# Deferred evictions and outputs of a squared-ReLU MLP tied in emission order; rows of the next block loaded further ahead

## The chip, the cores and the metric

One NeuronCore of one Trainium2 chip runs the whole layer. The metric is the device time of one execution in microseconds (us), as the median of the runs; less is better.

## What is computed

One step of a one-layer hybrid decoder in float32, for a prompt of 2048 tokens and for 8 x 8 sample tokens, 2112 rows in all. A token mixer (dilated attention, a Mamba-2 scan and a short gated convolution, with one input and one output projection) is followed by the MLP, the part that the change touches:

```python
x = x + rms_norm(mix, norm_mix_post[l])
h = rms_norm(x, norm_mlp_pre[l])
f = jnp.square(jax.nn.relu(h @ w_mlp_up[l])) @ w_mlp_down[l]   # 1024 -> 4096 -> 1024
x = x + rms_norm(f, norm_mlp_post[l])
```

## The kernel before

**Engines.** PE is the matrix engine (TensorE), DVE the vector engine, ACT the scalar engine, POOL the general engine GpSimd, SP the engine that only issues transfers. In the code they are `PE`, `V`, `A`, `G` and `SP`. Each works through its own instructions in order. The program is emitted by Python loops, and a scheduler then places the instructions of each engine; `tc.issue_after(ins)` keeps what is emitted under it behind `ins` in that placing. `Last` wraps an engine and remembers the last instruction emitted on it (`V.last`, `G.last`).

**Precision.** Every float32 operand is split in two rounded halves, `hi` and `lo`, and each product is made of three matmuls (hi·lo, lo·hi, hi·hi; `mm3`). So each weight tile costs ACT a cast (`whi`) and a subtraction (`wlo`: POOL's for up weights, DVE's for down weights), and each activation tile costs ACT a cast (`shi`) and DVE a subtraction (`slo`).

**Tiling.** The MLP runs from about 1340 us to the end, in three blocks of 704 rows. A block is two halves of 352 rows, each in three row pieces (128, 128 and 96 rows, p = 0 to 2). Up and down projections are each made by seven products in place of eight: first the up products in the order 1, 2, 6, 7, 5, 3, 4, then the down products in the order 1, 2, 7, 4, 5, 6, 3. Each product has eight steps (`jj`), 56 up and 56 down a block. An up step is 24 matmuls, 352 wide; a down step is 18 matmuls, 512 wide, two tiles `j` of nine: for each of the three banks wlo·shi and whi·shi, then three times whi·slo.

**One turn of the main loop** (a step `at`) emits the load of the weights four steps ahead (`w_load`, SP), the split of the weights one step ahead (`w_split`), a deferred piece of work if there is one (`late`), the activations of the next down step (`down_split`: DVE makes the combination `x`, then `shi` and `slo`), and then the matmuls of the step. The split weights lie in eight buffers, so the splits of a step wait until PE is done with the step two before it.

**At the end of a down product** its three PSUM banks (`pm`) are added into the output rows `Y` by DVE (`down_out`, rows y1 and y2 of the two halves): two additions a row piece for product 5, three for product 6. Where y2 is whole, ACT squares it (`jkf`, two a row piece) for the norm. For products 5 and 6 row piece 0 is done at once; row pieces 1 and 2 go to the list `late`, from which each turn takes one. `mlp_out` writes a finished row piece: POOL adds the sums of squares (`ssf`) and makes the reciprocal root (`rstd_ms`, `rstd`), DVE scales two halves of 512, POOL issues the transfer to `out_y_prompt`, which accumulates. y2 is written in steps 2 to 4 of product 3; y1 goes through `late` (`finish`) and is written in the first up steps of the next block.

**Rows of the next block.** The generator `half` has SP load three row tiles (`xt`), yields a number (a lead in us of PE's work), and then transposes them on PE (`pq`), with ACT copying each result (`q`). Transfers and transposes stand in between the steps as the streams are polled.

Of the kernel before, what the change touches and what calls it, by code (L numbers as in the profile page):

```python
# [2 lines left out]

# [1 line left out]

# [138 lines left out]
@with_exitstack  # L144
def hybrid_layer(ctx: ExitStack, tc: tile.TileContext, I, O, stage=9):
    nc = tc.nc
    V, A, G, PE, SP = Last(nc.vector), nc.scalar, Last(nc.gpsimd), TimedPE(nc.tensor), Last(nc.sync)

    cpool = ctx.enter_context(tc.tile_pool(name="const", bufs=1))
    dpool = ctx.enter_context(tc.tile_pool(name="scratch", bufs=1, space=DRAM))  # L150
# [150 lines left out]
    def y_rows(t0, n):  # L301
        if t0 < S:
            return O["y_prompt"][0, t0:t0 + n, :]
        return O["y_sample"].rearrange("b s d -> (b s) d")[t0 - S:t0 - S + n, :]
# [1303 lines left out]
    def s_pair(src):  # L1608

        hi = s4.tile([P, HT], F32R, name="shi", tag="s")  # L1610
        lo = s4.tile([P, HT], F32R, name="slo", tag="s")
        A.copy(hi, src)  # L1612
        V.tensor_sub(lo, src, hi.bitcast(F32))
        return hi, lo
# [109 lines left out]
    def up_sums(b):  # L1724

        (q11, q12), (q21, q22) = halves[b, 0].q, halves[b, 1].q

        def each(f):
            for c in range(4):
                with tc.issue_after(V.last):  # L1730
                    f(c)
                yield 3.0

        yield from each(lambda c: V.tensor_sub(q21[c], q21[c], q22[c]))
        while len(up_s.get((b, 1), [])) < 4:
            yield 1.0
        yield from each(lambda c: V.tensor_sub(q11[c], q21[c], q11[c]))
        src.update({(b, 6): q11, (b, 5): q21, (b, 4): q22})
        while len(up_s.get((b, 2), [])) < 4:
            yield 1.0  # L1740
        yield from each(lambda c: V.scalar_tensor_tensor(q12[c], q12[c], -1.0, q11[c], op0=ALU.mult,
                                                         op1=ALU.subtract))
        src[b, 3] = q12
# [16 lines left out]
    def down_split(b, i, j):  # L1760
        with tc.issue_after(V.last):
            a = down_form(i, j)
        down_s[b, i, j] = s_pair(a)

    def down_form(i, j):
        x = {k[:2]: v for k, v in X.items() if k[2] == j}
        if i == 1:
            a = x[1, 1]
        elif i == 2:
            a = x[1, 2]  # L1770
        elif i == 7:
            a = t4.tile([P, HT], F32, name="d3", tag="t")
            V.tensor_sub(a, x[1, 1], x[2, 1])
        elif i == 4:
            a = x[2, 2]
        elif i == 5:
            a = x[2, 1]
            V.tensor_sub(a, a, x[2, 2])
        elif i == 6:
            a = x[1, 1]  # L1780
            V.tensor_sub(a, x[2, 1], a)
        else:
            a = x[1, 2]
            V.scalar_tensor_tensor(a, a, -1.0, x[1, 1], op0=ALU.mult, op1=ALU.subtract)
        return a
# [36 lines left out]
    def mlp_out(b, t, p, last=False):  # L1822

        a, n = TP[p]
        t0 = BT * b + HT * (t - 1) + a
        y, ss = Y.pop((t, p)), SS.pop((t, p))
        G.tensor_add(ss[:n, 0:1], ss[:n, 0:1], ss[:n, 1:2])
        r = rstd_of(e4, ss[:, 0:1], n, D)
        for d in range(2):
            cs = slice(512 * d, 512 * d + 512)  # L1830
            o = y[:n, cs]
            if last and d == 0:
                A.activation(o, o, AF.Copy, scale=r[:n])
            else:
                with tc.issue_after(V.last):
                    V.scalar_tensor_tensor(o, o, r[:n], g4[:n, cs], op0=ALU.mult, op1=ALU.mult)
        for t1, t2 in ((t0, min(t0 + n, S)), (max(t0, S), t0 + n)):
            if t1 < t2:
                G.dma_start(y_rows(t1, t2 - t1), y[t1 - t0:t2 - t0], accum_op=ALU.add)
# [6 lines left out]
    def half(b, t):  # L1846
        h = halves[b, t] = Half(b, t, XT if b else [(y4, "y")])
        h.rows()
        yield 12.0
        yield from h.turn(psT, "tr")  # L1850

    def second_half(b):
# [3 lines left out]
    def next_block(b):  # L1856
        yield from half(b, 1)
        yield 6.0
        yield from half(b, 0)
        src[b, 1], src[b, 2] = halves[b, 0].q  # L1860
        yield from up_sums(b)

    late = []

# [3 lines left out]
    for at, (kind, b, i, jj) in enumerate(steps):  # L1868
        if at + 4 < len(steps):
            w_load(at + 4)  # L1870
        while nsplit[0] < len(steps) and nsplit[0] <= at + (2 if idle_y(nsplit[0]) else 1):
            w_split(nsplit[0])
            nsplit[0] += 1
        order = UP_ORDER if kind == "u" else DOWN_ORDER
        nxt = steps[at + 2] if at + 2 < len(steps) else None

        if kind == "u" and jj == NJ // 2 - 2 and i != UP_ORDER[-1]:
            ni = UP_ORDER[UP_ORDER.index(i) + 1]
            up_split(b, ni, (0, 1, 2))
        if kind == "d" and i == DOWN_ORDER[-1] and jj == NJ // 2 - 1 and (b + 1, 1) in src:  # L1880
            up_split(b + 1, 1, (0, 1, 2))
        if late:
            late.pop(0)()

        two = steps[at + 1] if at + 1 < len(steps) else None
        if two is not None and two[0] == "d" and kind == "d":
            for j2 in range(2):
                down_split(two[1], two[2], 2 * two[3] + j2)
        if kind == "u":
            hi, lo = wts.pop(at)  # L1890
            s = up_s[b, i]
            for j2 in range(2):
                ps = bank()
                for c in range(4):
                    ws = slice(2 * P * c + P * j2, 2 * P * c + P * j2 + P)
                    mm3(ps[:, :HT], hi[:, ws], lo[:, ws], *s[c], c == 0, c == 3)
                up_out(i, 2 * jj + j2, ps)
        else:
            hi, lo = wts.pop(at)
            if jj == 0:  # L1900
                banks = [bank() for _ in TP]
            for j2 in range(2):
                j = 2 * jj + j2
                s = down_s.pop((b, i, j))
                ws = slice(512 * j2, 512 * j2 + 512)
                for p, (a, n) in enumerate(TP):
                    mm3(banks[p][:n], s[0][:, a:a + n], s[1][:, a:a + n], hi[:, ws], lo[:, ws], j == 0, j == NJ - 1)
            if jj == NJ // 2 - 1:
                for p in range(len(TP)):
                    if i in (5, 6) and p:  # L1910
                        late.append(lambda i=i, p=p, ps=banks[p]: end_tile(i, p, ps))
                    else:
                        end_tile(i, p, banks[p])
        if two is not None and two[0] == "d" and kind == "u":
            for j2 in range(2):
                down_split(two[1], two[2], 2 * two[3] + j2)
        if kind == "u" and jj == NJ // 2 - 1 and i != UP_ORDER[-1]:
            up_split(b, UP_ORDER[UP_ORDER.index(i) + 1], (3,))
        if kind == "d" and i == DOWN_ORDER[-1] and jj == NJ // 2 - 1 and b + 1 < TT // BT:
            while (b + 1, 1) not in src:  # L1920
                advance(min(streams, key=lambda st: st[1]))
            have = len(up_s.get((b + 1, 1), []))
            up_split(b + 1, 1, range(have, 4))
        if kind == "d":
            end, last = jj == NJ // 2 - 1, b == TT // BT - 1
            if i == 2 and end and last:
                for p in range(len(TP)):
                    o = Y[1, p][:TP[p][1], :512]
                    V.tensor_mul(o, o, g4[:TP[p][1], :512])
            if i == 3 and not end and 2 <= jj < 2 + len(TP):  # L1930
                mlp_out(b, 2, jj - 2)
            if i == 3 and end:
                def finish(p, b=b, last=last):
                    square(1, p, 2)
                    mlp_out(b, 1, p, last)
                for p in range(len(TP)):
                    if last:
                        finish(p)
                    else:
                        late.append(lambda p=p, f=finish: f(p))  # L1940
        if kind == "d" and i == 5 and jj == 4 and b + 1 < TT // BT:
            stream(next_block(b + 1))
        if at % 20 == 10 and shifts:
            nm, sr, sb_ = shifts.pop(0)
            with tc.issue_after(wload[0].ins):
                SP.dma_start(O[nm][0, sb_, 0:WB - NS].rearrange("t h e -> t (h e)"),
                                  I[sr][0, sb_, NS:WB].rearrange("t h e -> t (h e)"))
        poll()
# [38 lines left out]
```

## Time and profile before

| | us |
|---|---|
| runs | 2785.82, 2782.39, 2784.89 |
| median | 2784.89 |
| the profiled execution: its time | 2779.39 |
| its span, first to last instruction | 2777.6 |
| PE busy | 2577.4 (93%) |
| DVE, ACT, POOL busy | 1509.1, 1328.9, 1087.9 |
| mean granted TensorE clock | 0.969 |

All numbers of the profile are from that one execution, which lies 5.5 us below the median of the runs. The views used are the page of the profile (busy time of each engine), the same in chosen stretches of time, the waits of an engine with what ended each of them, and the timeline of single instructions. A timeline row has start and duration in us, engine, line, operation, the tile written and those read, the shape, a count where several like ones are joined, and in brackets the idle time before it with what released it. Matmuls are pipelined, so one shown with 0.39 us can follow another after 0.23 us.

### The profile page before, as it was taken

What the parts mean: (1) busy time and instruction counts of PE and PEld (TensorE: products, weight loads), DVE (VectorE), ACT (ScalarE), POOL (GpSimd) and SP (SyncE); (2) the same over time, 40 slices, a digit from 0 to 9 for tenths busy, and PEclk for the clock granted to TensorE, in tenths of its full rate; (3) what the DMA queues carried; (4) which work ended last, traced back from release to release, by engine and by line L of the source; (5) the groups of instructions that cost most, each with busy time, mean ns of one, the idle gap of its engine ahead of it and who ended that gap; (6) DMA issues with size and microseconds to landing.
All of it is one profiled execution on the core that took longest, in us unless ns stands there. A gap on an engine that the chain in (4) does not pass through costs nothing. (4 is left out here: it accounts for less than half of the span.)

```text
span 2777.6 us, 40701 instructions
## 1 busy us (share of the span) xinstructions
PE 2577.4 (93%) x14329; PEld 2182.4 (79%) x14329; DVE 1509.1 (54%) x2994; ACT 1328.9 (48%) x2776; POOL 1087.9 (39%) x1008
## 2 busy tenths in 40 slices
PE   7998889989999878999999999999999999999996
PEld 6898767877877755556799977689987779998775
DVE  4555536455456465554154466754546674445676
ACT  4534334435436333334456644454764455385443
POOL 4545444444354544434577300066610017660002
PEclk9999899999999988999999999999999999999998
DMA  7777998777677649978776545374534456543343
GB/s 206 221 184 225 271 245 241 202 212 217 182 212 198 163 134 285 279 225 265 239 234 203 151 155 169 127 228 167 167 122 153 131 161 210 167 160 132 125 152 87
DMA packets 426260, 528.26 MB, mean 190 GB/s; under 512 B 65482, under 2 KB 326130, under 8 KB 421448
## 3 DMA queue, kind: packets, MB, share of 16 engines
q1 hardware_dynamic: 411352, 483.45, 54.7%
q0 software_dynamic: 14704, 42.21, 9.1%
q8 instruction: 113, 1.85, 0.3%
q14 instruction: 91, 0.75, 0.1%
HBM read 447.90 MB, written 178.19 MB: 225 GB/s over the span
## 5 line engine op out<-in xcount | busy, mean ns | idle before, releaser
L137 POOL TENSOR_TENSOR wlo<-wraw,whi 128x512 fp32r<-128x512 f32 (+2 forms) x359 | 675.5, 1909 | 522.2 <-ACT whi L417 292.6
L1604 ACT CAST whi<-wraw 128x1024 fp32r<-128x1024 f32 x336 | 351.8, 1049 | 334.4 <-PE pm L118 272.2
L118 PE MATMUL pm<-slo,whi 128*128 128x352 f32 x1344 | 436.0, 326 | 7.9 <-DVE x2t L137 3.5
L118 PE MATMUL pm<-shi,wlo 128*128 128x352 f32 x1344 | 432.2, 327 | 8.6 <-POOL wlo L137 8.6
L118 PE MATMUL pm<-shi,whi 128*128 128x352 f32 x1344 | 437.3, 325 | 0.0
L118 PE MATMUL pm<-wlo,shi 128*128 128x512 f32 (+1 forms) x1008 | 398.7, 396 | 1.0 <-ACT shi L1612 1.0
L118 PE MATMUL pm<-whi,shi 128*128 128x512 f32 (+1 forms) x1008 | 397.9, 395 | 0.0
L118 PE MATMUL pm<-whi,slo 128*128 128x512 f32 (+1 forms) x1008 | 340.1, 400 | 19.9 <-DVE slo L137 19.8
L137 DVE TENSOR_TENSOR wlo<-wraw,whi 128x1024 fp32r<-128x1024 f32 (+1 forms) x169 | 206.2, 1220 | 206.3 <-ACT whi L1604 192.6
L118 PE MATMUL pj<-lo,whi 128*128 128x512 f32 (+1 forms) x720 | 272.1, 378 | 17.6 <-ACT xr L631 8.2
L118 PEld LDWEIGHTS pm<-slo,whi 128*128 128x128 f32 x1344 | 255.5, 190 | 10.7 <-ACT whi L1604 4.0
L118 PE MATMUL pj<-hi,whi 128*128 128x512 f32 (+1 forms) x720 | 262.9, 365 | 0.0
L118 PEld LDWEIGHTS pm<-shi,wlo 128*128 128x128 f32 x1344 | 254.7, 190 | 9.4 <-POOL wlo L137 9.4
L118 PE MATMUL pj<-hi,wlo 128*128 128x512 f32 (+1 forms) x720 | 261.8, 364 | 0.0
L137 POOL TENSOR_TENSOR ssf<-ssf 128x1 f32<-128x1 f32 (+1 forms) x18 | 9.1, 503 | 643.0 <-ACT jkf L1820 642.8
L118 PEld LDWEIGHTS pm<-shi,whi 128*128 128x128 f32 x1344 | 255.4, 190 | 0.2
L137 DVE TENSOR_TENSOR x<-pm,x 128x352 f32<-128x352 f32 x240 | 123.7, 521 | 235.7 <-PE pm L118 235.4
L118 PEld LDWEIGHTS pm<-whi,slo 128*128 128x128 f32 (+1 forms) x1008 | 179.8, 181 | 75.7 <-DVE slo L137 26.4
L118 PEld LDWEIGHTS pm<-wlo,shi 128*128 128x128 f32 (+1 forms) x1008 | 182.3, 181 | 56.1 <-ACT shi L1612 4.1
L118 PEld LDWEIGHTS pm<-whi,shi 128*128 128x128 f32 (+1 forms) x1008 | 181.7, 180 | 51.2 <-issue 0.2
L1612 ACT CAST shi<-x 128x352 fp32r<-128x352 f32 x288 | 136.8, 484 | 164.9 <-DVE x L137 112.2
L137 DVE TENSOR_TENSOR slo<-x,shi 128x352 fp32r<-128x352 f32 x288 | 156.7, 554 | 35.8 <-ACT shi L1612 30.6
(324 smaller groups left out, 4856.9 us busy)
## 6 DMA issues: line engine op xcount, KB each, us to landing
wraw<-in_w_in SPq DMA_DIRECT2D x192, 256.0 KB
wraw<-u_d SPq DMA_DIRECT2D x96, 512.0 KB
wraw<-d_d SPq DMA_DIRECT2D x96, 512.0 KB
wraw<-in_w_mlp_up SPq DMA_DIRECT2D x72, 512.0 KB
wraw<-in_w_mlp_down SPq DMA_DIRECT2D x72, 512.0 KB
u_d<-in_w_mlp_up POOLq DMA_DIRECT2D x64, 256.0 KB, 5.7
d_d<-in_w_mlp_down POOLq DMA_DIRECT2D x64, 256.0 KB, 7.0
out_s_k<-in_cache_attn_k SPq DMA_DIRECT2D x8, 2040.0 KB
```

What stands on the lines that cost most here:

```text
L118: return self.eng.matmul(out, lhsT, rhs, **kw)
L137: out = f(*args, **kw)
L1604: A.copy(hi, raw)
L1612: A.copy(hi, src)
```

## The change

Four edits. The remembered last instruction is now kept for ACT too. The deferred work `late` is taken after `down_split` of the next step instead of before it, and everything that it emits is placed behind the last instructions emitted on DVE, ACT and POOL (`in_order`). The outputs of y2 are bound in the same way. And `half` yields 18 us in place of 12 between the loads and the transposes.

```diff
-    V, A, G, PE, SP = Last(nc.vector), nc.scalar, Last(nc.gpsimd), TimedPE(nc.tensor), Last(nc.sync)
+    V, A, G, PE, SP = Last(nc.vector), Last(nc.scalar), Last(nc.gpsimd), TimedPE(nc.tensor), Last(nc.sync)
...
         h.rows()
-        yield 12.0
+        yield 18.0
...
+    @contextmanager
+    def in_order():
+
+        with tc.issue_after(V.last), tc.issue_after(A.last), tc.issue_after(G.last):
+            yield
...
-        if late:
-            late.pop(0)()
 
         two = steps[at + 1] if at + 1 < len(steps) else None
         if two is not None and two[0] == "d" and kind == "d":
             for j2 in range(2):
                 down_split(two[1], two[2], 2 * two[3] + j2)
+        if late:
+            with in_order():
+                late.pop(0)()
...
             if i == 3 and not end and 2 <= jj < 2 + len(TP):
-                mlp_out(b, 2, jj - 2)
+                with in_order():
+                    mlp_out(b, 2, jj - 2)
```

The set of instructions is the same in both kernels; their order on the engines is not. SP's order is the same, and so are the places of the transposes on PE. Three places differ in the second half of each block.

DVE from product 5 to product 6 of block 0. Before (y are the evictions of product 5, x11 and slo the activations of product 6, wlo4 its weights; `slo_17684` is the second tile of its first step):

```order
L137 TENSOR_TENSOR y2_17155<-y2_17155,pm_17440 128x512
L137 TENSOR_TENSOR y1_16585<-y1_16585,pm_17440 128x512
L137 TENSOR_TENSOR x11_14399<-x21_15069,x11_14399 128x352
L137 TENSOR_TENSOR wlo4_17710<-wraw4_17603,whi4_17709 128x1024
L137 TENSOR_TENSOR y2_17157<-y2_17157,pm_17441 96x512
L137 TENSOR_TENSOR y1_16587<-y1_16587,pm_17441 96x512
L137 TENSOR_TENSOR slo_17684<-x11_14370,shi_17683 128x352
```

And now, from the same place:

```order
L137 TENSOR_TENSOR wlo4_17710<-wraw4_17603,whi4_17709 128x1024
L137 TENSOR_TENSOR x11_14387<-x21_15069,x11_14387 128x352
L137 TENSOR_TENSOR slo_17684<-x11_14356,shi_17683 128x352
L137 TENSOR_TENSOR slo_17715<-x11_14387,shi_17714 128x352
L137 TENSOR_TENSOR x11_14404<-x21_15084,x11_14404 128x352
L137 TENSOR_TENSOR wlo4_17749<-wraw4_17637,whi4_17748 128x1024
L137 TENSOR_TENSOR x11_14434<-x21_15106,x11_14434 128x352
L137 TENSOR_TENSOR slo_17720<-x11_14404,shi_17719 128x352
L137 TENSOR_TENSOR y2_17155<-y2_17155,pm_17440 128x512
L137 TENSOR_TENSOR y1_16585<-y1_16585,pm_17440 128x512
```

The four evictions of row pieces 1 and 2 moved from ahead of that slo to behind those of the next two steps (the two of row piece 0 stand ahead of it in both).

DVE from product 6 to product 3. Before (`slo_18007` is the second tile of product 3's first step, `slo_18058` the first of its second):

```order
L137 TENSOR_TENSOR y2_17153<-pm_17725,y2_17153 128x512 x2
L137 TENSOR_TENSOR y1_16583<-pm_17725,y1_16583 128x512
L137 TENSOR_TENSOR y2_17155<-pm_17726,y2_17155 128x512 x2
L137 TENSOR_TENSOR y1_16585<-pm_17726,y1_16585 128x512
L137 SCALAR_TENSOR_TENSOR x12_14051<-x12_14051,x11_14399 128x352
L137 TENSOR_TENSOR y2_17157<-pm_17727,y2_17157 96x512 x2
L137 TENSOR_TENSOR y1_16587<-pm_17727,y1_16587 96x512
L137 TENSOR_TENSOR wlo4_18045<-wraw4_17914,whi4_18044 128x1024
L137 SCALAR_TENSOR_TENSOR x12_14087<-x12_14087,x11_14446 128x352
L137 TENSOR_TENSOR slo_18007<-x12_14023,shi_18006 128x352
L137 TENSOR_TENSOR slo_18058<-x12_14051,shi_18057 128x352
```

And now, where these two tiles are `slo_18001` and `slo_18044`:

```order
L137 TENSOR_TENSOR y2_17153<-pm_17725,y2_17153 128x512 x2
L137 TENSOR_TENSOR y1_16583<-pm_17725,y1_16583 128x512
L137 TENSOR_TENSOR wlo4_18039<-wraw4_17908,whi4_18038 128x1024
L137 SCALAR_TENSOR_TENSOR x12_14051<-x12_14051,x11_14387 128x352
L137 TENSOR_TENSOR slo_18001<-x12_14023,shi_18000 128x352
L137 TENSOR_TENSOR wlo4_18090<-wraw4_17948,whi4_18089 128x1024
L137 TENSOR_TENSOR slo_18044<-x12_14051,shi_18043 128x352
L137 SCALAR_TENSOR_TENSOR x12_14066<-x12_14066,x11_14404 128x352
L137 SCALAR_TENSOR_TENSOR x12_14087<-x12_14087,x11_14434 128x352
L137 TENSOR_TENSOR slo_18049<-x12_14066,shi_18048 128x352
L137 TENSOR_TENSOR y2_17155<-pm_17726,y2_17155 128x512 x2
L137 TENSOR_TENSOR y1_16585<-pm_17726,y1_16585 128x512
```

Six evictions left the way of `slo_18001`, and the weights of the third step (`wlo4_18090`) came ahead of `slo_18044`.

ACT at the same place, now (`whi4_18089` are the weights of the third step, `shi_18043` is the first tile of the second; before, four squares stood ahead of that shi, and this whi behind it):

```order
L137 CAST whi4_18038<-wraw4_17908 128x1024
L137 CAST shi_18000<-x12_14023 128x352
L137 ACTIVATE jkf_18026,ssf_18025<-y2_17153 128x512
L137 ACTIVATE jkf_18028,ssf_18025<-y2_17153 128x512
L137 CAST whi4_18089<-wraw4_17948 128x1024
L137 CAST shi_18043<-x12_14051 128x352
L137 CAST shi_18048<-x12_14066 128x352
L137 CAST shi_18094<-x12_14087 128x352
L137 ACTIVATE jkf_18056,ssf_18055<-y2_17155 128x512
```

Here too the squares of row pieces 1 and 2 moved back, and a whi moved ahead of a shi.

POOL at the start of block 1, where y1 of block 0 is written between the weight splits of the first up product (`wlo4_18471` belongs to its third step, `wlo4_18517` to its fourth). Before:

```order
L137 TENSOR_TENSOR ssf_16855<-ssf_16855 128x1
L137 TENSOR_TENSOR ssf_16859<-ssf_16859 128x1
L137 TENSOR_SCALAR rstd_ms_18431<-ssf_16855 128x1
L137 TENSOR_TENSOR ssf_16863<-ssf_16863 96x1
L137 TENSOR_SCALAR rstd_ms_18477<-ssf_16859 128x1
L137 TENSOR_TENSOR rstd_18432<-rstd_ms_18431,mhalf_117 128x1
L137 TENSOR_SCALAR rstd_ms_18523<-ssf_16863 96x1
L137 TENSOR_TENSOR rstd_18478<-rstd_ms_18477,mhalf_117 128x1
L137 TENSOR_TENSOR rstd_18524<-rstd_ms_18523,mhalf_117 96x1
L137 TENSOR_TENSOR wlo4_18471<-wraw4_18295,whi4_18470 128x1024
L137 DMA out_y_prompt<-y1_16583 128x1024
L137 TENSOR_TENSOR wlo4_18517<-wraw4_18336,whi4_18516 128x1024
```

And now:

```order
L137 TENSOR_TENSOR ssf_16855<-ssf_16855 128x1
L137 TENSOR_SCALAR rstd_ms_18431<-ssf_16855 128x1
L137 TENSOR_TENSOR rstd_18432<-rstd_ms_18431,mhalf_117 128x1
L137 TENSOR_TENSOR wlo4_18471<-wraw4_18295,whi4_18470 128x1024
L137 TENSOR_TENSOR ssf_16859<-ssf_16859 128x1
L137 DMA out_y_prompt<-y1_16583 128x1024
L137 TENSOR_SCALAR rstd_ms_18477<-ssf_16859 128x1
L137 TENSOR_TENSOR wlo4_18517<-wraw4_18330,whi4_18516 128x1024
L137 TENSOR_TENSOR rstd_18478<-rstd_ms_18477,mhalf_117 128x1
L137 TENSOR_TENSOR ssf_16863<-ssf_16863 96x1
L137 TENSOR_SCALAR rstd_ms_18523<-ssf_16863 96x1
L137 TENSOR_TENSOR rstd_18524<-rstd_ms_18523,mhalf_117 96x1
```

The norms of row pieces 1 and 2 moved behind the splits of the third and fourth step; the other two transfers stood between the two splits before, and now stand behind the split of the fifth step (`wlo4_18563`).

More of the change, by code (lines that the diff above doesn't have):

```diff
@@ L1 @@
 import math
-from contextlib import ExitStack
+from contextlib import ExitStack, contextmanager
 import numpy as np
```

## The prediction

> **What bounds the kernel.** I read the page first, then stretches of 50 us, then TensorE's waits, then the timelines where it waits. In the rows by stretch, the five pairs after the length are busy time and instructions of PE, PEld, DVE, ACT and POOL; then come the granted TensorE clock, the DMA share and GB/s.
>
> ```profile
> PE 2577.4 (93%) x14329; PEld 2182.4 (79%) x14329; DVE 1509.1 (54%) x2994; ACT 1328.9 (48%) x2776; POOL 1087.9 (39%) x1008
> ```
>
> ```profile
> 1650.00:1700.00 50.00, 49.97 (x218) 38.56 (x217) 31.17 (x48) 22.78 (x36) 0.00 (x0) 1.00 0.42 127
> ...
> 1750.00:1800.00 50.00, 45.91 (x190) 35.29 (x190) 36.95 (x63) 23.81 (x43) 5.64 (x9) 0.93 0.32 107
> 1800.00:1850.00 50.00, 44.51 (x227) 39.83 (x226) 32.06 (x48) 25.78 (x45) 30.12 (x23) 0.93 0.75 205
> 1850.00:1900.00 50.00, 50.00 (x313) 50.00 (x312) 22.72 (x38) 30.90 (x56) 32.64 (x14) 1.00 0.70 231
> ```
>
> TensorE (PE) is the bound: 93% of the span, and 49.97 or 50.00 of 50 us where nothing disturbs it. There it issues a 512-wide down matmul every 50/218 = 0.23 us, a 352-wide up matmul every 50/313 = 0.16 us. Only time in which it waits, or runs at a lower granted clock (0.93), can be won. From 1600 us to the end it waits, by releaser (total, times, longest):
>
> ```profile
> PE pm L118 <- DVE slo L137: 19.8, 8, 4.1
> PE pm L118 <- POOL wlo L137: 6.9, 2, 3.4
> PE pq L122 <- DMA xt<-xn_d: 4.8, 3, 2.1
> PE pm L118 <- ACT whi L1604: 2.9, 3, 1.2
> PE pm L118 <- ACT shi L1612: 1.0, 3, 0.4
> ```
>
> Three places hold nearly all of it: products 5 to 6, products 6 to 3, and the start of the next block.
>
> **Products 5 to 6 (three times).** First and last of three:
>
> ```profile
> 1745.60 0.40 PE L118 MATMUL pm<-whi,shi 128*96 128x512 f32 x1
> 1747.63 0.96 PE L118 MATMUL pm<-whi,slo 128*128 128x512 f32 x3 [1.64 <-DVE slo L137]
> ...
> 2689.27 0.96 PE L118 MATMUL pm<-whi,slo 128*128 128x512 f32 x3 [2.32 <-DVE slo L137]
> ...
> 1741.90 2.48 DVE L137 TENSOR_TENSOR y<-y,pm 128x512 f32<-128x512 f32 x4 [1.69 <-PE pm L118]
> ...
> 1745.87 1.27 DVE L137 TENSOR_TENSOR y<-y,pm 96x512 f32<-96x512 f32 x2
> 1747.06 0.51 DVE L137 TENSOR_TENSOR slo<-x,shi 128x352 fp32r<-128x352 f32 x1
> ```
>
> Before, six y evictions stand ahead of this slo; after, two. Four go: 4 x 0.62 = 2.5 us (2.48/4 each). The slo is then done about 2.4 us earlier, near 1745.2, and PE wants it at 1745.60 + 0.23 = 1745.8. The waits of 1.6 to 2.3 us go; those evictions return behind slo tiles with a whole step (18 x 0.23 = 4.1 us) of cover. I take 5.7 us for all three, 6.3 at most.
>
> **Products 6 to 3 (three times).**
>
> ```profile
> 1780.56 0.39 PE L118 MATMUL pm<-whi,shi 128*96 128x512 f32 x1
> 1785.04 1.65 PE L118 MATMUL pm<-whi,slo 128*128 128x512 f32 x3 [4.09 <-DVE slo L137]
> 1786.49 0.63 PE L118 MATMUL pm<-wlo,shi 128*128 128x512 f32 x1
> ...
> 1790.24 0.40 PE L118 MATMUL pm<-wlo,shi 128*128 128x512 f32 x1
> ...
> 2726.66 1.65 PE L118 MATMUL pm<-whi,slo 128*128 128x512 f32 x3 [4.08 <-DVE slo L137]
> ...
> 1777.08 3.08 DVE L137 TENSOR_TENSOR y<-pm,y 128x512 f32<-128x512 f32 x5 [0.26 <-PE pm L118]
> ...
> 1781.11 1.88 DVE L137 TENSOR_TENSOR y<-pm,y 96x512 f32<-96x512 f32 x3
> 1782.90 1.21 DVE L137 TENSOR_TENSOR wlo<-wraw,whi 128x1024 fp32r<-128x1024 f32 x1
> 1784.04 0.51 DVE L137 SCALAR_TENSOR_TENSOR x<-x,x 128x352 f32<-128x352 f32 x1
> 1784.47 0.95 DVE L137 TENSOR_TENSOR slo<-x,shi 128x352 fp32r<-128x352 f32 x2
> ...
> 1779.65 0.63 ACT L1820 ACTIVATE jkf<-y 128x512 bf16<-128x512 f32 x1 [0.22 <-DVE y L137]
> ...
> 1781.22 0.49 ACT L1612 CAST shi<-x 128x352 fp32r<-128x352 f32 x1
> ...
> 1784.15 1.05 ACT L1604 CAST whi<-wraw 128x1024 fp32r<-128x1024 f32 x1 [0.79 <-DVE wlo L137]
> ```
>
> PE is 1785.04 - 1780.56 - 0.23 = 4.25 us late. From 1785.04 to 1790.24 it then issues 12 matmuls in 5.2 us where 12 x 0.23 = 2.8 are due: 2.4 us more, the price of the halved clock (0.63 each instead of 0.39). Together 6.65 us a time, 19.9 for three.
> After: three y from 1777.08 (to 1778.9), wlo of step 1 (1.2), x (0.45), slo done near 1781.0: three evictions (1.88), three more (1.8) and nothing else leave its path, and ACT's shi (1781.22 before, behind four squares) comes earlier for the same reason. PE wants this slo at 1780.8: 0.2 us late. Next, ACT converts step 2's whi (1.05 us, held until the fifth shi matmul near 1780.7) ahead of the shi that step 1 opens with: ready 1780.7 + 1.05 + 0.45 = 2.2 past 1780, and PE is there at 1781.0 + 0.69 = 1.7: 0.6 us late. The evictions and squares (jkf, 0.63 here) of row pieces 1 and 2 are late next; they pass behind the slo tiles of steps 1 and 2, and one square stands ahead of a later whi and shi: 0.2, by the same count. Together 1.0, each part below the 2.32 us that the clock survived. I take 6.65 - 1.0 = 5.65 x 3 = 17.0 us.
>
> The Trainium skill (TensorE: Matmul & The Clock Gate, Part 1) says the clock halves after an idle window of about 3.4 us and recovers after about 3.4 busy ones. The first half agrees with the rows here: 3.43 and more halved it, 2.32 did not. By its recovery time a halving would cost 3.4/2 = 1.7 us, an estimate from that page, and the whole sum 3.5 us less over five; the row says 2.4, and decides.
>
> **Start of blocks 1 and 2 (twice).**
>
> ```profile
> 1829.03 0.66 PE L118 MATMUL pm<-shi,wlo 128*128 128x352 f32 x1 [3.43 <-POOL wlo L137]
> ...
> 2303.35 0.66 PE L118 MATMUL pm<-shi,wlo 128*128 128x352 f32 x1 [3.44 <-POOL wlo L137]
> ...
> 1820.13 0.48 POOL L137 TENSOR_TENSOR ssf<-ssf 128x1 f32<-128x1 f32 x1
> ...
> 1823.73 0.56 POOL L137 TENSOR_TENSOR rstd<-rstd_ms,mhalf 128x1 f32<-128x1 f32 x1
> ...
> 1826.64 2.33 POOL L137 TENSOR_TENSOR wlo<-wraw,whi 128x1024 fp32r<-128x1024 f32 x1
> 1828.92 0.93 POOL L137 DMA_DIRECT2D out_y_prompt<-y  x1
> ...
> 1824.33 1.42 DVE L137 SCALAR_TENSOR_TENSOR y<-y,rstd,gpost 128x512 f32<-128x512 f32 x2 [1.27 <-POOL rstd L137]
> 1826.18 5.32 DVE L137 SCALAR_TENSOR_TENSOR y<-y,rstd,gpost 128x512 f32<-128x512 f32 x4 [0.44 <-POOL rstd L137]
> ```
>
> Before, wlo of step 2 starts at 1826.64, behind all three norms; wait and slow clock cost 3.43 + 2.4 = 5.9 us, and a 0.85 us whi wait follows (among the 2.9). After, only the first norm stands ahead: ssf ends 1820.6, rstd_ms and rstd are done by about 1821.7, whi is ready near 1822.1: it waits for the end of step 0, which PE reaches 28 matmuls (4.5 us) before the 1825.4 at which it wants this wlo (four matmuls into step 2), and the rest of a copy (0.2) and its own 1.05 follow. So wlo ends by 1822.1 + 2.33 = 1824.4, 1 us early, and that wait goes with its slow clock.
> But the out DMA of row piece 0 now stands ahead of wlo of step 3, on POOL's one queue, and waits for two DVE scalings. Four scalings took 5.32 us where 2 x 1.42 = 2.84 are due; wlo (2.33) ran in between: DVE stood still for it. So after wlo ends at 1824.4, DVE does four 352-wide ones (1.8) and two scalings (1.42): 1827.6; DMA 0.93, a small rstd_ms, wlo 2.33: 1831.4. Due is 1825.4 + 24 x 0.16 = 1829.3: 2.1 us late. Were DVE not held, the DMA would go at about 1825 and this wlo would be in time. Behind it in POOL's queue stand only the later norms and splits; PE alone waits for those. The later splits stand behind rstd, ssf, rstd and behind two DMAs: about 0.5 and 0.8, estimates from the same rows. I take 3.0 (between 0.5 and 3.4, nearer the 5.32 row): 6.75 - 3.0 = 3.75, twice 7.5 us.
>
> The Trainium skill (SBUF — State Buffer, "SBUF: two separate sides") speaks against the change here: GpSimd and two-input DVE instructions take one port pair in turn, each for its whole instruction. The 5.32 row agrees; without that rule this term would be about 4 us better.
>
> **The rest.** Longer lead of the rows, 12 to 18: SyncE's order and the transposes' places are the same in both kernels, so the xt waits (4.8) stay: 0. In block 0 some weight-sum DMAs pass behind weight splits on POOL, ahead of the one 1.73 us wlo wait (below): 0 to 2, I take 0.4. Scalings and outputs of y2 fall where POOL has idle time: 0. No instruction is added or dropped.
>
> **Sum.** 5.7 + 17.0 + 7.5 + 0.4 = 30.6 us. The profiled execution took 2779.39 us (span 2777.6), so 2748.8. The runs' median is 2784.89, 5.5 above it: 2754.
>
> **Rivals.**
> (a) The new wait at the block's start grows past 3.4 us and halves the clock again. For it: 2.1 needs only 1.3 more, and a shorter wait has done it once:
>
> ```profile
> 1367.17 0.96 PE L122 MATMUL pq<-cst,xt 128*128 128x128 f32 x6
> ...
> 1369.86 0.43 PE L118 MATMUL pm<-shi,wlo 128*128 128x352 f32 x1 [1.73 <-POOL wlo L137]
> ...
> 1370.29 0.49 PE L118 MATMUL pm<-shi,whi 128*128 128x352 f32 x1
> ```
>
> Against: that one came straight behind six short transposes, the 2.32 ones behind full matmuls. Price: 3.4 + 2.4 for the wait and its clock, 1.3 for the two splits behind it, 7.1 a time against 6.75, so that term is nothing: 2754 + 7.5 = 2762. Chance 0.21.
> (b) At 6 to 3 the wait moves one step on and stays over 3.4 us, since ACT's whi and DVE's wlo now lead. It needs 2.8 us more than I find; then that term is nothing: 2771. With (a): 2778. Chance 0.08.
> (c) It does not do what it says: PE waits as long for something else (weights landing late, the outputs' traffic): 2779 to 2790. For it: the DMA share is highest at the block's start (0.75, 0.70). Against: at that same 0.70 the row from 1850 has PE full, so weights come in time at full rate. Chance 0.07.
> (d) Slower: out DMAs behind scalings behind wlo hold POOL so long that three splits of each block's start wait over 3.4 us, each with a halved clock: 3 x 5.9 = 17.7 against 6.75, +11 a time, +22 in all, which the other 23 just balance; at 5 us each (+31) it is slower, about 2793. It decides where one DMA waits 5 us for its scalings; 1826.18 shows 2.5. Chance 0.05.
> The forecast, 2745 to 2761, has 0.59.
>
> Differences of under 0.2% (5.6 us) can't be told from none here. Faster: forecast, (a) and (b), 0.88; same: (c), 0.07; slower: (d), 0.05. Range: with all gains whole, 6.3 + 19.9 + 13.5 + 2 = 42, it would be 2743; the top takes in (a) and (b), 2771, and 2 us of scatter between executions (the runs lie 3.4 apart), 2773, and leaves (c), (d) and both together outside.
>
> **What would show it.** Right: slo waits drop from 19.8 to under 5 us, none over 3; PEclk near 1.00 in 1750 to 1850 (shifted some us); one wlo wait of 1 to 3 us at the fourth step of each block; xt unchanged. Wrong: a wait over 3.4 us with 0.63 us matmuls behind it at either place, or PE idle before shi at step 1 of product 3.

## Result and profile after

The change takes 2769.2 us (median; 2755.3 to 2775.9) where the kernel before, run beside it, takes 2785.6 (2782.4 to 2786.7): ratio 0.9936, 95% interval 0.9912 to 0.996. It gains 16 us, about half of the 30.6 of the forecast's sum; the time lies inside the range, and above the 2745 to 2761 that the forecast gave to its likeliest case. The profiled execution took 2772.1 us (span 2770.3).

First the three stretches around the first two places (the columns are those of before), then TensorE's waits from 1600 us to the end:

```profile
1750.00:1800.00 50.00, 49.67 (x215) 37.46 (x214) 43.38 (x73) 25.47 (x47) 1.70 (x3) 1.00 0.39 128
1800.00:1850.00 50.00, 43.82 (x226) 36.70 (x224) 41.25 (x47) 25.26 (x45) 32.01 (x29) 1.00 0.80 218
1850.00:1900.00 50.00, 49.05 (x288) 49.05 (x289) 27.15 (x38) 30.31 (x57) 29.44 (x12) 0.93 0.63 208
```

```profile
PE pm L118 <- ACT whi L137: 5.9, 2, 3.4
PE pm L118 <- POOL wlo L137: 5.2, 4, 2.0
PE pm L118 <- DVE slo L137: 3.2, 5, 1.0
PE pq L122 <- DMA xt<-xn_d: 2.3, 2, 1.4
```

Read against before: the slo waits fell from 19.8 us (longest 4.1) to 3.2 (longest 1.0), and 1750 to 1800 went from 45.91 to 49.67 us busy at the full granted clock. Before, that stretch holds 6 to 3 alone (the wait at 5 to 6 ends at 1747.63); now it holds both, since the part ahead took longer in this execution. The stretch from 1800 did not improve (44.51 busy before, 43.82 now), and the granted clock of 0.93 moved from there to the stretch from 1850, where before TensorE was full. The wlo waits went only from 6.9 to 5.2, and whi waits doubled from 2.9 to 5.9, of which one is 3.4. (ACT's rows are those of line 137 now, inside `Last`, which wraps ACT too.)

**Why the time has to be split.** The spans differ by 2777.6 - 2770.3 = 7.3 us, less than the 16 of the medians. Both kernels have the same order ahead of the MLP, up to a 3.48-us wait for x2t with which it begins. Its row before, and after:

```profile
1341.02 0.66 PE L118 MATMUL pm<-slo,whi 128*128 128x352 f32 x1 [3.48 <-DVE x2t L137]
```

```profile
1349.36 0.66 PE L118 MATMUL pm<-slo,whi 128*128 128x352 f32 x1 [3.48 <-DVE x2t L137]
```

The part ahead took 8.3 us longer in the profiled execution of the change. From that row to the end of the span it is 1436.6 us before and 1420.9 after: 15.7 less, which is what the medians say (16.4). Below, "the MLP" is that stretch, start row to end of span. It can be cut further, since TensorE's instructions are the same ones in both kernels, in the same order but for a few matmuls that stand some places off: the time between the same two places in that order is compared. Differences to the profile of before, in us (minus is a gain), summed over the three blocks; the starts are two, each with the last step of product 3 ahead of it. What lies behind the last matmul is in the MLP alone, and where a cut falls within a step moves up to 0.4 us between neighbouring columns:

| kernel | first up and down products | 5 to 6, with the xt waits ahead | 6 to 3 | rest of product 3 | block starts | sum | MLP |
|---|---|---|---|---|---|---|---|
| forecast | -0.4 | -5.7 | -17.0 | 0 | -7.5 | -30.6 | 1406.0 |
| before, again | +1.3 | -1.7 | -0.4 | 0 | -0.2 | -1.1 | 1435.4 |
| the change | +1.3 | -9.9 | -16.4 | +5.8 | +3.3 | -15.8 | 1420.9 |
| the change, again | +1.8 | -9.8 | -16.4 | +6.5 | +1.3 | -16.6 | 1419.7 |

The two terms that were forecast at 5 to 6 and 6 to 3 came. Two things did not: the rest of product 3 loses 6 us where nothing was forecast, and the block starts win nothing where 7.5 were.

**6 to 3 now.** Block 0, TensorE and DVE:

```profile
1786.32 0.39 PE L118 MATMUL pm<-whi,shi 128*96 128x512 f32 x1
1786.78 0.96 PE L118 MATMUL pm<-whi,slo 128*128 128x512 f32 x3
...
1788.01 0.50 PE L118 MATMUL pm<-wlo,shi 128*128 128x512 f32 x1 [0.27 <-ACT shi L137]
...
1782.83 1.89 DVE L137 TENSOR_TENSOR y<-pm,y 128x512 f32<-128x512 f32 x3 [0.25 <-PE pm L118]
1784.64 1.22 DVE L137 TENSOR_TENSOR wlo<-wraw,whi 128x1024 fp32r<-128x1024 f32 x1
...
1786.20 0.52 DVE L137 TENSOR_TENSOR slo<-x,shi 128x352 fp32r<-128x352 f32 x1
```

Three evictions, wlo and the activations are left between the end of product 6 and its successor's slo. TensorE goes from whi·shi to whi·slo in 1786.78 - 1786.32 = 0.46 us instead of 4.48, and the matmuls stay 0.96 for three: no halved clock. The next wait is 0.27, for ACT's shi, as forecast (0.6 there, though 2.2 less 1.7, its own terms, make 0.5).

**The rest of product 3.** Some 20 us on, same block, TensorE, DVE, POOL:

```profile
1806.52 0.40 PE L118 MATMUL pm<-whi,shi 128*96 128x512 f32 x1
1807.45 0.73 PE L118 MATMUL pm<-whi,slo 128*128 128x512 f32 x2 [0.54 <-DVE slo L137]
...
1805.55 1.42 DVE L137 SCALAR_TENSOR_TENSOR y<-y,rstd,gpost 128x512 f32<-128x512 f32 x2 [1.01 <-POOL rstd L137]
...
1806.88 0.52 DVE L137 TENSOR_TENSOR slo<-x,shi 128x352 fp32r<-128x352 f32 x1
...
1803.43 0.93 POOL L137 DMA_DIRECT2D out_y_prompt<-y  x1 [16.29 <-DVE x L137]
...
1804.96 0.56 POOL L137 TENSOR_TENSOR rstd<-rstd_ms,mhalf 128x1 f32<-128x1 f32 x1
```

POOL is idle for 16.29 us before its first out transfer: it does have the time that the forecast saw. But tied in order, the norm of row piece 1 stands behind the transfer of piece 0, and that transfer behind DVE's two scalings. So DVE comes to its next scalings before their rstd, stands still 1.01 us, and the slo behind them reaches TensorE 0.54 us late.

**Start of block 1.** POOL, DVE, TensorE, SP's queue and ACT:

```profile
1824.68 3.04 POOL L137 TENSOR_TENSOR wlo<-wraw,whi 128x1024 fp32r<-128x1024 f32 x1 [0.75 <-ACT whi L137]
...
1830.29 0.94 POOL L137 DMA_DIRECT2D out_y_prompt<-y  x1 [2.13 <-DVE y L137]
...
1838.60 0.90 POOL L137 DMA_DIRECT2D out_y_prompt<-y  x1
1840.16 0.82 POOL L137 DMA_DIRECT2D out_y_prompt<-y  x1 [0.66 <-DVE y L137]
...
1825.38 2.72 DVE L137 TENSOR_TENSOR q<-q 128x352 f32<-128x352 f32 x1
...
1833.96 0.43 PE L118 MATMUL pm<-shi,wlo 128*128 128x352 f32 x1 [1.97 <-POOL wlo L137]
...
1842.08 0.37 SPq L137 DMA_DIRECT2D wraw<-in_w_mlp_up  x1
...
1848.91 1.99 ACT L137 CAST whi<-wraw 128x1024 fp32r<-128x1024 f32 x2 [3.10 <-DMA wraw<-in_w_mlp_up]
...
1850.95 0.66 PE L118 MATMUL pm<-slo,whi 128*128 128x352 f32 x1 [3.38 <-ACT whi L137]
1851.41 0.50 PE L118 MATMUL pm<-shi,whi 128*128 128x352 f32 x1
```

The wlo part came as forecast: the 3.43-us wait is gone, and the split behind the transfer is 1.97 us late (2.1 forecast), the next two 0.62 and 0.63 (0.5 and 0.8). DVE's row at 1825.38, 2.72 us for a 352-wide operation (0.5 otherwise) while wlo runs on POOL, is the hold that the forecast counted with. What it lacked is in the last four rows: a weight load issued at 1842.08 is in ACT's hands only at 1848.91, 6.8 us later; ACT stands 3.10 us for it and TensorE 3.38, with the lower clock behind it (0.93 in the stretch from 1850; the first two matmuls, 1850.95 and 1851.41, are 0.46 us apart). Before, y1's last two transfers started at 1830.48 and 1831.80, which is 13.4 and 14.7 us behind the block's first matmul (1817.10); now they start at 1838.60 and 1840.16, 19.0 and 20.5 behind it (1819.62), next to that load.

### The profile page after: what moved, and what is told of

Its sections match the earlier page's. It is cut to its first block, busy times and chain, and to the rows that moved or that the text cites. A ratio compares the mean times of both kernels' runs of the same rounds, so it can differ in the third digit from the quotient of the medians.

```text
span 2770.3 us, 40697 instructions
## 1 busy us (share of the span) xinstructions
PE 2583.0 (93%) x14329; PEld 2183.1 (79%) x14329; DVE 1533.3 (55%) x2994; ACT 1327.3 (48%) x2776; POOL 1085.4 (39%) x1008
## 3 DMA queue, kind: packets, MB, share of 16 engines
q8 instruction: 113, 1.85, 0.3%
## 5 line engine op out<-in xcount | busy, mean ns | idle before, releaser
L137 ACT CAST whi<-wraw 128x1024 fp32r<-128x1024 f32 (+2 forms) x528 | 468.9, 892 | 410.0 <-PE pm L118 262.9
L137 ACT ACTIVATE x<-x 128x352 f32<-128x352 f32 x384 | 183.3, 495 | 43.9 <-DVE x L137 39.3
```

Of the source, the lines that this page charges most:

```text
L137: out = f(*args, **kw)
```

## Experiments

**1. Does the difference stand when both kernels run again?** The change unaltered, and the kernel before unaltered; the question was also where the 8 us ahead of the MLP come from.

> The changed kernel, unaltered, profiled and timed once more. Marker: the matmul that ends the 3.48 us wait for x2t at the MLP's start (1341.02 us in the profile before, 1349.36 in that of the change); from it to the end of the span 1436.6 and 1420.9 us. Theory A (the part ahead of the marker, whose order is the same in both kernels, varies from execution to execution by about 10 us): marker anywhere from 1340 to 1360, from the marker to the end 1421 within 3 us, times spread over 10 us or more. Theory B (the change lengthens that part for good): marker 1349 within 2 us again, and that of the kernel before at 1341 within 2.

> The kernel before, unaltered, profiled and timed once more. Theory A: marker not at 1341 but somewhere in 1341 to 1351, from the marker to the end 1436.6 within 3 us. Theory B: marker 1341 within 2 us, 1436.6 after it.

The change: 2762.6 us against 2779.3 beside it, ratio 0.9935 (0.9919 to 0.995). Before, again: ratio 1.0002 (0.9988 to 1.0016). The MLP takes 1419.7 and 1435.4 us, as in the first profiles (table above). Where it starts:

```profile
1345.48 0.66 PE L118 MATMUL pm<-slo,whi 128*128 128x352 f32 x1 [3.48 <-DVE x2t L137]
```

```profile
1340.19 0.43 PE L118 MATMUL pm<-slo,whi 128*128 128x352 f32 x1 [3.48 <-DVE x2t L137]
```

So 1349.4 and 1345.5 for one kernel, and 1341.0 and 1340.2 for the other; over the 13 profiles of this study it lies between 1340.2 and 1350.4. It does not go with the change's edits: a kernel below with all of them and later transfers has 1340.9, and what the timed medians hold besides the MLP is the same for both kernels in each comparison (1348.3 and 1349.0, then 1342.9 and 1343.6). The part ahead scatters by 10 us from one execution to the next, so kernels are compared below by the MLP's time, with the timed ratio beside it.

**2. Are the ties behind the loss in product 3?** The outputs of y2 untied, all else as in the change:

```diff
-                with in_order():
-                    mlp_out(b, 2, jj - 2)
+                mlp_out(b, 2, jj - 2)
```

> The change without the binding of y2's outputs (mlp_out of y2 outside in_order); only POOL's order differs from the change, where the three norms come ahead of the three transfers again. Theory (the change loses 2.0 us a block in product 3, because DVE's scalings wait for rstd, which stands on POOL behind a transfer that waits for the scaling before it, with slo queued behind): the slo waits at product 3's later steps (0.54, 0.50, 0.97 and 0.54 us in the change) go, from the marker to the end 1415 within 2 us, 6 less than the change's 1420.9, ratio to the kernel before near 0.992. Rival (those losses are the price of the late evictions themselves): the waits stay, 1421.

And, run later, the outputs of y2 still tied, but two steps on, when the late evictions are done:

```diff
-            if i == 3 and not end and 2 <= jj < 2 + len(TP):
+            if i == 3 and not end and 4 <= jj < 4 + len(TP):
                 with in_order():
-                    mlp_out(b, 2, jj - 2)
+                    mlp_out(b, 2, jj - 4)
```

> The change with y2's outputs in steps 4 to 6 of product 3 in place of 2 to 4. Theory S (DVE is short of time there: six late evictions and six scalings, 0.62 and 0.7 us each, fall into the first five steps, where a step leaves it about 1.2 us): with the scalings moved back, the loss in product 3 (2.1, 2.2 and 1.6 us by block) falls under 1 us a block; from the marker to the end 1416.5 within 2 us. Rival R (DVE waits for rstd behind POOL's transfers wherever the outputs stand): the slo waits of 0.5 to 1 us move to later steps and stay, 1420 within 1.5.

Untied, the rest of product 3 loses 1.3, 1.3 and 1.6 us a block: 4.1 instead of 5.8 and 6.5. (MLP 1417.8, ratio 0.994, 0.9918 to 0.9961.) Its waits, in the same view as above (TensorE from 1600 us, here the row of slo), keep their longest:

```profile
PE pm L118 <- DVE slo L137: 2.5, 5, 1.0
```

Two steps later, the loss is gone where it stood: -0.56 in block 2, and +0.22 and +0.21 in blocks 0 and 1 up to the last step. So most of it is a lack of time on DVE: six evictions and six scalings fall into the first steps, and the ties, with DVE waiting for POOL's norms, are about a third of it. But in blocks 0 and 1 the last step of product 3 now loses 1.74 and 1.76 us, so that all of product 3 behind 6 to 3 still loses 1.96 and 1.97 there (2.1 and 2.2 in the change). The last step of block 0, DVE and TensorE:

```profile
1812.60 1.42 DVE L137 SCALAR_TENSOR_TENSOR y<-y,rstd,gpost 128x512 f32<-128x512 f32 x2 [1.01 <-POOL rstd L137]
...
1815.49 2.69 DVE L137 TENSOR_TENSOR slo<-x,shi 128x352 fp32r<-128x352 f32 x1 [0.61 <-ACT shi L137]
...
1818.24 0.95 PE L118 MATMUL pm<-whi,slo 128*128 128x512 f32 x3 [1.07 <-DVE slo L137]
```

The scaling stands 1.01 us for its rstd, as long as in the change, and the last slo takes 2.69 us in place of 0.52 while POOL splits weights of the next block (1815.14 to 1817.79). So the rival of the second expectation, that the waits move with the outputs, holds for this part. The start of block 2 got worse by 3.3 us as well, with one new wait (TensorE from 1600 us):

```profile
PE pm L118 <- ACT x L137: 3.3, 1, 3.3
```

The kernel as a whole won only 3 to 4 us over the change's two profiles (MLP 1416.6, ratio 0.9948, 0.9933 to 0.9963).

**3. Are the block starts lost to the transfers?** y1's transfers of blocks 0 and 1 made a sixty-fourth as large, at the same place (the rest of these rows is left out of the output):

```diff
+                c1 = 16 if t == 1 and not last else D
-                G.dma_start(y_rows(t1, t2 - t1), y[t1 - t0:t2 - t0], accum_op=ALU.add)
+                G.dma_start(y_rows(t1, t2 - t1)[:, :c1], y[t1 - t0:t2 - t0, :c1], accum_op=ALU.add)
```

> The change with only 16 of 1024 columns of y1's outputs of blocks 0 and 1 written (the rest of these rows is left out); instructions and, but for a few neighbours, their order stay. Theory T (the whi waits of 3.38 and 2.50 us at the start of blocks 1 and 2 come from weight loads that share the DMA engines with y1's outputs, which now go out later): both waits fall under 1.2 us, no halved clock there, from the marker to the end about 1411, 10 less; the wlo waits of 2.0 us stay. Rival Q (the loads are issued late, in a chain of POOL's splits and PE's last use of a buffer, whatever the traffic): the whi waits stay at 2.5 to 3.4, 1421 within 2 us.

The whi wait at block 1 falls from 3.38 to 1.34 us, that at block 2 from 2.50 to 0.23, and the first two matmuls behind it are 0.27 us apart, not 0.46 (timeline of this kernel, TensorE):

```profile
1847.97 0.42 PE L118 MATMUL pm<-slo,whi 128*128 128x352 f32 x1 [1.34 <-ACT whi L137]
1848.24 0.32 PE L118 MATMUL pm<-shi,whi 128*128 128x352 f32 x1
```

The block starts win 3.9 and 3.7 us, 7.6 in all, against a loss of 3.3 and 1.3 in the two profiles of the change. The load itself is not issued late: it goes 22.5 us behind the block's first matmul in the change and 22.2 here, and is in ACT's hands 6.8 us later there (7.7 in the second run) and 3.8 here; the same load took at most 3.8 before. So that it comes late is due to the y1 output that moves beside it. The wlo waits are a little shorter too (1.18 and 1.14 us at both blocks, against 1.97, 0.62 and 0.63 at block 1 and 2.00 at block 2). The MLP's 1415.6 is above the expected, since the xt waits (3.8 us in this execution, 2.3 in the change) took 3 us of it; ratio 0.9918 (0.9898 to 0.9938).

**4. Only the evictions tied.** y1's finish and y2's outputs left to the scheduler as before:

```diff
-            with in_order():
-                late.pop(0)()
+            tied, f = late.pop(0)
+            if tied:
+                with in_order():
+                    f()
+            else:
+                f()
...
-                        late.append(lambda i=i, p=p, ps=banks[p]: end_tile(i, p, ps))
+                        late.append((True, lambda i=i, p=p, ps=banks[p]: end_tile(i, p, ps)))
...
-                with in_order():
-                    mlp_out(b, 2, jj - 2)
+                mlp_out(b, 2, jj - 2)
...
-                        late.append(lambda p=p, f=finish: f(p))
+                        late.append((False, lambda p=p, f=finish: f(p)))
```

> Only the late evictions of products 5 and 6 are tied; the outputs of y1 and y2 are free, so POOL's order at the start of blocks 1 and 2 is that of the kernel before. From the marker (end of the 3.48 us wait for x2t) to the end, the kernel before took 1436.6 and 1435.4 us, the change 1420.9 and 1419.7. Theory (all of the gain is in the evictions, about 2.5 us a block at products 5 to 6 and 5.4 at 6 to 3; tying the outputs costs 1.5 to 2 us at each block's start and about 1 in product 3): the 3.4 us wlo wait at each block's start is back, and still 1416 within 2.5 us, less than the change. Rival (tying the outputs gains as predicted, 3.75 us a block's start): 1424 or more.

TensorE's waits from 1600 us in this kernel:

```profile
PE pm L118 <- POOL wlo L137: 8.1, 2, 4.0
PE pm L118 <- ACT whi L137: 2.8, 3, 1.2
```

The two wlo waits of before are back (4.0 each), the whi waits are those of before (2.9 there), and 5 to 6 and 6 to 3 keep their gain (-9.5, -16.3). MLP 1414.1, ratio 0.9942 (0.9924 to 0.996). So tying the finish of y1 trades the wlo wait for the whi wait and brought nothing; the whole gain of the change is that of its evictions. By times alone the two can't be told apart.

**5. The transfers later.** As the change, but each transfer of y1 is held back: by this code it is emitted two turns after its scalings, where the expectation says one. So that of row piece 0 stands behind the norm of piece 1 and its weight split:

```diff
...
+                if not last:
+                    held = []
+                    def turn0(f=finish, held=held):
+                        f(0, hold=held)
+                    def turn1(f=finish, held=held):
+                        f(1, hold=held)
+                    def turn2(f=finish, held=held):
+                        held.pop(0)()
+                        f(2, hold=held)
+                    def turn3(held=held):
+                        held.pop(0)()
+                    late.extend([turn0, turn1, turn2, turn3, turn3])
```

> The change with each of y1's three transfers emitted one turn after its scaling, so that on POOL it stands behind the weight split that it held up. Theory (the wlo waits of 2.0, 0.6 and 0.6 us come from transfers that wait for DVE's scalings ahead of the splits, DVE being held by POOL's split before): these waits fall under 0.5 us at both block starts; the whi wait behind them (2.0 to 4.3 in the change) stays, since the transfers still meet the weight loads; from the marker to the end 1414 within 2.5 us. Rival (the splits wait for ACT's whi or PE's release of their buffers): the waits stay, 1420.

The same view of this kernel:

```profile
PE pm L118 <- ACT whi L137: 3.6, 3, 2.5
...
PE pm L118 <- POOL wlo L137: 1.3, 5, 0.3
```

The wlo waits fall from 5.2 to 1.3 us in all, none over 0.31: the split no longer stands behind a transfer that waits for scalings. The whi waits stay partly (2.51 and 0.67). Block starts -7.5, MLP 1410.6, better than expected; 2756.3 us, ratio 0.9911 (0.9891 to 0.9931).

**6. The lead of the rows back to 12.**

```diff
-        yield 18.0
+        yield 12.0
```

> The change with 12 us in place of 18 between loads and transposes of rows. Theory (this edit moves no load and no transpose; the xt waits differ between executions of one kernel): xt waits from 1600 us on between 2 and 5 us, from the marker to the end 1420.5 within 2 us, ratio to the kernel before within 0.002 of the change's. Rival (the longer lead is worth 2 us or more): 1423 or more and xt waits of over 4.5 us.

The same view again:

```profile
PE pm L118 <- POOL wlo L137: 4.3, 6, 1.0
PE pq L122 <- DMA xt<-xn_d: 3.5, 3, 1.5
```

xt waits of 3.5 us, inside what the profiles with 18 show (2.3 to 3.8); ratio 0.9935 (0.9918 to 0.9952), MLP 1418.0. One of these waits does go with the lead: for rows in the last step of product 5 of block 0 TensorE stands 0.57 to 0.73 us in all four profiles with 12 (before twice, this one, experiment 8), and with 18 in one of nine (0.41). Loads and transposes stand at the same places in all; how the lead acts on it was not followed up. It has another side: with 12 the long wlo waits are 0.92 and 1.01 (one split earlier) instead of 2.0, since the combinations of the new rows (q on DVE, the 2.72-us row above) no longer stand ahead of y1's scalings there.

**7. What does the work: the move, or the ties?** The deferred work taken after `down_split` but not tied (both `in_order()` removed), and tied but taken ahead of `down_split`, as before:

> The change with nothing tied: the deferred work is still taken after down_split, but in_order is gone from both places. Theory (the place in the emission alone does nothing, since the scheduler lifts the evictions ahead of the activations again; the binding is what works): the slo waits of 4 us at products 6 to 3 are back with the halved clock, from the marker to the end 1436 within 3 us, ratio to the kernel before between 0.998 and 1.003. Rival (taking it later is enough): 1420 to 1425.

> The change with the deferred work tied, but taken before down_split as in the kernel before. On DVE three evictions of row piece 1 (1.9 us) then stand ahead of the slo that PE waits for at products 6 to 3, and two (1.25) at 5 to 6. Theory (each eviction ahead of that slo costs its 0.62 us, and the clock halves only where the wait passes about 3.4 us): waits of 2.0 us at 6 to 3 and 0.6 at 5 to 6, no halved clock at either; product 6 to 3 about 3.5 to 4 us better a block than before in place of 5.4; from the marker to the end 1425 within 2.5 us. Rival (a wait of 2 us halves the clock as well): 1431 or more.

The slo waits of the one that is moved and not tied, then the timeline of TensorE at 6 to 3 (block 0) and the slo waits of the one that is tied and not moved:

```profile
PE pm L118 <- DVE slo L137: 16.6, 8, 3.7
```

```profile
1784.29 0.96 PE L118 MATMUL pm<-whi,slo 128*128 128x512 f32 x3 [1.86 <-DVE slo L137]
...
1785.43 0.39 PE L118 MATMUL pm<-whi,shi 128*128 128x512 f32 x1
```

```profile
PE pm L118 <- DVE slo L137: 13.4, 13, 1.9
```

Untied (first row), the move alone leaves slo waits of 3.65, 3.62 and 3.65 at 6 to 3, since the scheduler puts the evictions ahead again. Behind each the matmuls are 0.43 us apart in place of 0.23, but for 8, 14 and 6 of them: a halved clock does not always cost the 2.4 us of the forecast. Ratio 0.9995 (0.9983 to 1.0007): no change; the MLP's 1430.9 is 5 us below the expected. Tied but ahead (the other rows), the waits at 6 to 3 are 1.86, 1.89 and 1.85 and the clock stays (0.39 behind them): 0.9977 (0.9961 to 0.9994), MLP 1423.8. So 6 to 3 wins 2.5 us by the move alone, 9.6 by the tie alone, 16.4 by both.

**8. The parts that helped, together.** Evictions and finish tied, transfers of y1 later (as in 5), y2's outputs untied, lead 12:

> Evictions tied and y1's transfers one turn after their scaling (as in e6_dma_later), y2's outputs free (as in e3_out2_free), 12 us of lead (as in e8_yield12). If the three gains add: from the marker to the end e6's 1410.6 less 1.8 in product 3 (e3 against the change) less up to 3 at the block starts and in block 0: 1407 within 3 us, ratio to the kernel before near 0.990, below the change's 0.9935. If they meet in the same waits: 1410 to 1412, as e6.

Its waits:

```profile
PE pm L118 <- ACT whi L137: 4.2, 3, 2.0
...
PE pm L118 <- POOL wlo L137: 2.0, 2, 1.0
```

2755.5 us against 2778.9 beside it, ratio 0.9913 (0.9898 to 0.9928); MLP 1410.7. It beats both kernels, but not experiment 5 alone (1410.6): the gains met in the same waits, and the rest of product 3 (+4.2) and the whi waits stay.

The same table for all of them:

| kernel | first products | 5 to 6 | 6 to 3 | rest of 3 | block starts | MLP |
|---|---|---|---|---|---|---|
| y2's outputs untied | +1.9 | -9.1 | -16.3 | +4.1 | +1.4 | 1417.8 |
| y2's outputs two steps later | -0.4 | -9.4 | -16.2 | -0.1 | +6.4 | 1416.6 |
| y1's transfers small | +2.7 | -6.6 | -16.2 | +5.7 | -7.6 | 1415.6 |
| evictions alone tied | 0 | -9.5 | -16.3 | +4.0 | -0.7 | 1414.1 |
| y1's transfers later | +1.9 | -9.8 | -16.3 | +5.9 | -7.5 | 1410.6 |
| lead 12 | +1.4 | -8.5 | -16.2 | +5.8 | -0.8 | 1418.0 |
| moved, not tied | +0.6 | -4.0 | -2.5 | -0.5 | +1.0 | 1430.9 |
| tied, not moved | -1.3 | -3.6 | -9.6 | +2.9 | -1.0 | 1423.8 |
| the best parts | +0.7 | -8.8 | -16.2 | +4.2 | -5.7 | 1410.7 |

## Why the prediction was right, and where not

- **Sign and main mechanism: right.** Six and four evictions left the way of a slo tile; TensorE was waiting for just these. 6 to 3 gave 16.4 us of the 17.0 forecast, with the 2.4 us per halved clock in it. Experiment 7 shows that it needs both the tie and the move.
- **Products 5 to 6: right, with more on top.** 9.9 and 9.8 instead of 5.7, in a stretch that holds the xt waits as well. In the steps of the three slo waits alone (1.64, 2.32 and 2.32 before) it is 1.93, 2.61 and 2.61, 7.15 in all and more than the 6.3 given as the most; where the 0.3 beyond each wait comes from was not looked into. Of the rest, 0.86 is in the step of the xt wait that goes with the lead (experiment 6), and 1.7 is also in the second run of before, where nothing changed.
- **Longer lead, 0: nearly right.** One xt wait of 0.6 to 0.7 us goes with it; against that, the wlo waits are longer with 18 than with 12 (experiment 6).
- **"Start of blocks 1 and 2", 7.5 us: wrong, the first failed step.** It measured a loss of 3.3 and of 1.3. The working on POOL's queue held (2.1, 0.5 and 0.8 us forecast, 1.97, 0.62 and 0.63 found). The omission was that "PE alone waits" behind the moved transfers: they compete with the weight loads (experiment 3), and moved by 5.6 and 5.8 us against the block's start, the last two met the load that ACT needs next. The forecast had noted that this stretch has the highest DMA share, and set it aside because 1850 to 1900 ran full at 0.70; that row was from an order in which y1's transfers were already through. With small transfers (experiment 3) the term is 7.6, near the 7.5 forecast. In price it is close to rival (a), by which this term is nothing; of that rival's mechanism a part came: the new wlo wait never passed 2.0 us, but in one of its four places, block 2 of the first profile, the clock fell behind it (last section), as the rival's row of 1.73 us had warned.
- **"Scalings and outputs of y2 fall where POOL has idle time: 0": wrong, the second.** It measured a loss of 5.8 and of 6.5. POOL had the time; DVE had not, and the step counted the late evictions' cover (4.1 us a step) without the scalings that fall into the same steps, nor what the ties make DVE wait for POOL. Two steps later the loss is gone in those steps, but blocks 0 and 1 lose nearly as much in the last one (experiment 2).
- **Weight sums in block 0, -0.4:** +1.3 and +1.8, but +1.3 as well in before's second run: not a result.
- **From the sum to the time.** With the means of the change's two profiles: 30.6 less 9.8 (the starts, +2.3 for -7.5), less 6.1 (product 3), plus 4.1 (5 to 6), less 1.9 (first products) and 0.6 (6 to 3) leaves 16.3, and the medians differ by 16.4 and 16.7. The time lies in the range by the room that was left for rivals (a) and (b), not by the sum: half of the gain was lost at two places, and one of them, product 3, is in none of the rivals.

## What to carry to other kernels

When deferred work is tied behind an engine's order, list for every issue in it what it waits for and what then stands behind it, on every queue, and add the transfers: a transfer moved by a few us is moved into another load's time. Cover counted for one kind of moved work has to be counted against all the work that is moved into the same steps. A scheduler left free may undo a move in the code altogether, so the order on the engines is read, not the code.

## What the runs showed of the hardware

Between 2 and 3.6 us the length of a wait does not decide whether the clock falls behind it. In the change, block 2, TensorE:

```profile
2303.32 0.43 PE L118 MATMUL pm<-shi,wlo 128*128 128x352 f32 x1 [2.00 <-POOL wlo L137]
...
2305.91 0.50 PE L118 MATMUL pm<-slo,whi 128*128 128x352 f32 x1
2306.20 0.50 PE L118 MATMUL pm<-shi,whi 128*128 128x352 f32 x1
```

A wait of 2.00 us is followed, from 2304.23 to 2307.67, by 3.4 us of matmuls 0.29 us apart (2305.91, 2306.20) where 0.16 is due; the granted clock is 0.50 there. In the second run of the change nearly the same wait was not, and with y2's outputs two steps later not even one of 3.58 us:

```profile
2300.78 0.43 PE L118 MATMUL pm<-shi,wlo 128*128 128x352 f32 x1 [1.98 <-POOL wlo L137]
2301.04 0.32 PE L118 MATMUL pm<-slo,whi 128*128 128x352 f32 x1
```

```profile
1851.06 0.43 PE L118 MATMUL pm<-slo,whi 128*128 128x352 f32 x1 [3.58 <-ACT whi L137]
1851.33 0.32 PE L118 MATMUL pm<-shi,whi 128*128 128x352 f32 x1
```

Nor were the waits of 2.32 before. The prediction took 2.32 us as survived and 3.43 as enough; by these rows a wait of 2 us carries some chance of a slow stretch behind it, and one of 3.58 some chance of none. The Trainium skill (TensorE: Matmul & The Clock Gate, Part 1) says that the window by which the clock is switched is free-running, and that the point of the switch to full speed depends on where in it the first matmul lands. Two like waits with unlike outcomes fit that, but no run here changes the place of a wait alone, so it is not shown as the cause.

The other surprise is the scatter ahead of the MLP: the same instructions in the same order on every engine took 1340.2 to 1349.4 us up to the first row of the MLP in the four profiles of the two kernels, more than most of the differences looked for. What sets it was not tried and stays open.
